# Down projections of a hybrid encoder layer: pair 17 multiplied in seven block products in the first run too, with its token sums made ahead of that run's eighth pair and the run's order rearranged

## The chip, the cores and the metric

The kernel runs on one core of one Trainium2 chip. The metric is the device time of one execution, in microseconds (us). The profile comes from one further execution of the same program, whose span is measured from the trace and whose own time is given beside it. Engines are named as the profile names them: PE multiplies matrices (PEld is its weight load), DVE and ACT are the vector and the scalar engine, POOL and SP issue DMA transfers here.

## The reference, cut to what matters

The layer has two feed-forward blocks of one form, one at its beginning and one at its end, and the change touches the second matrix product (the "down projection") of both.

```python
def swiglu(x, w_gate_up, w_down):
    gate, up = jnp.split(x @ w_gate_up, 2, axis=-1)
    return (jax.nn.silu(gate) * up) @ w_down
...
ff = swiglu(rms_norm(x, pre_norm_ffn1[layer]), w_ffn1_gate_up[layer], w_ffn1_down[layer])
x = x + 0.5 * rms_norm(ff, post_norm_ffn1[layer])
```

There are 256 tokens, the model width is 2048 and the hidden width is 5632, all in float32. So `w_down` is 5632 x 2048 and the product has 256 x 2048 results. Between the two feed-forward blocks lie a gated linear recurrence and a windowed attention, which the change leaves alone.

## The kernel before, in words

**Three products for one.** A float32 operand is split into a high part and a low part (`h` and `l`): ACT casts the tile to the high part (L177) and DVE subtracts it from the original to get the low part (L178). One product of two blocks is then three matmuls (high by high, high by low, low by high), which `Blocks.three` issues. All of them stand at line L458 in the profile. Each multiplies 128 x 128 weights into 512 columns.

**Pairs and runs.** `hts` holds the hidden activations: 22 tiles ("pairs"), each of two 128-row slices, already split into high and low. The down projection is done in two runs over these 22 pairs: run 0 makes the output columns 0 to 1023, run 1 the columns 1024 to 2047. For each pair and run, one raw tile of `w_down` (2 x 128 rows by 1024 columns, 1024 KB) is loaded, split and multiplied. The order of the pairs is written out by hand in the table `orders` (L1276), one list for each run. A place in that list is called a position here; position 6 is the seventh pair of a run, and pair 12 stands there.

**Plain and seven.** A pair is a 2 x 2 block of activations by a 2 x 2 block of weights. A plain pair takes eight block products, so 24 matmuls; its raw tile is split in two halves (two casts on ACT, two subtractions on DVE). A pair "in seven" takes seven block products, so 21 matmuls, by a scheme of the Strassen kind (`Blocks.products`, L505). It needs sums of the activation blocks ("token sums", tile `sums` or `su`, split into `sp`), and sums of the weight blocks in place of some weight blocks. Its first block is split alone (`ha`, `la`, from `one_block`, three of them at a time), then the lower half, then two weight sums are made on DVE (L1342 and L1343), then the upper half and once more the lower half are split (here "upper" and "last").

**Where the other weight sums come from.** For a pair listed in the table `added` (L1281), `prepare` (L1310) is called four positions ahead: it splits the first block and then has POOL issue a transfer of 512 KB (L1314) which adds the right-hand weight blocks onto the raw tile in flight. A pair in seven that is not in `added` makes these sums on DVE (L1337).

**Token sums.** Pairs 0, 2, ..., 18 are `MIXED`, and go in seven in both runs. For pairs 0 to 14 the token sums are made in the stage before. For 16 and 18, `sums_again` (L1103) makes them during run 0, after the products of positions 8 and 14. It is five instructions on DVE (L1107, and four small ones L1111 to L1114). Pair 17 is plain in run 0; its sums are made after the products of index 24, that is the third pair of run 1, and it goes in seven in run 1 alone.

**Raw tiles and their loads.** Five raw tiles go round. When a pair's last half is split, `load_down` (L1293, transfer L1298 on SP) fills the tile with the next pair of a list that is sorted by position, with pairs of `added` pulled forward by 3.5 positions (L1283). Eight activation tiles (pairs 0 to 7) were put away in device memory in the stage before and are fetched back into four slots (`fetch`, L1139) at fixed positions (`fetch_at`).

**The order on the engines.** The whole stage is under a manual schedule: each engine runs its instructions as the code writes them. Step i of the loop at L1401 writes the split of position i + 1, then `prepare` of position i + 4 and the fetches, then the products of position i, then the rest of the split, then token sums due there. So DVE and ACT work ahead of PE; five `h` tiles and five `l` tiles (`hip`, `lop`) bound by how much.

Of the kernel before, what the change touches and what calls it, by code (L numbers as in the profile page):

```python
# [37 lines left out]
def hymba_layer_kernel(  # L38
# [37 lines left out]
    def nm(s):  # L76
        uid[0] += 1
        return f"{s}_{uid[0]}"
# [120 lines left out]
    def close_far():  # L199
        far["cm"].__exit__(None, None, None)  # L200
# [719 lines left out]
    def post_pool():  # L920
        return tc.tile_pool(name=nm("post"), bufs=4, reuse_waits="tile")
# [17 lines left out]
    MIXED = range(0, 20, 2)  # L939
# [142 lines left out]
    def ffn(gated, w_dn, post_gain, again, gain=None, lead=None, aside=None):  # L1082

        with ExitStack() as st:
# [6 lines left out]
            hts, sums, away = [], {}, {}  # L1091
# [98 lines left out]
            def some(steps, n):  # L1190
                for _ in range(n):
                    next(steps)
# [47 lines left out]
            def first_pairs(g, waiting):  # L1240

                gated.group(g)
                some(waiting, 1)
                gated.prepare(g, MIXED_IN[1])
                some(waiting, 1)
                ahead = gated.splits(g, 1)
                some(ahead, 2)
                gated.prepare(g, MIXED_IN[2])
                for one in gated.take(g, 0):
                    one()  # L1250
                some(waiting, 1)
                ahead = gated.splits(g, 2)
                some(ahead, 2)
                some(waiting, 1)
                some(ahead, 1)
                for one in gated.take(g, 1):
                    one()

            def pair_ahead(g, u):

                ahead = gated.splits(g, u + 1)
                next(ahead)
                if u + 1 == MIXED_IN[1]:
                    gated.prepare(g, MIXED_IN[3])
                next(ahead)
                for one in gated.take(g, u):
                    one()
                for _ in ahead:
                    pass
                if g == 1 and u == 5:  # L1270
                    sums_in(MIXED_IN[3])
                if u == 5 and 1 < g <= AWAY // 2 + 1:
                    put_away(2 * g - 4)
                    put_away(2 * g - 3)

            orders = [  # L1276
                [9, 11, 8, 13, 10, 15, 12, 1, 0, 3, 14, 5, 16, 17, 2, 7, 4, 19, 6, 18, 20, 21],

                [2, 7, 4, 9, 6, 8, 11, 10, 13, 12, 17, 15, 0, 5, 14, 3, 16, 1, 18, 19, 20, 21],
            ]  # L1280
            added = {0: (12, 0, 14, 16, 2, 4, 6, 18), 1: (*MIXED, 17)}  # L1281
            steps = [(r, u) for r in range(2) for u in orders[r]]
            in_order = sorted(  # L1283
                (i - 3.5 if u in added[r] else i, i) for i, (r, u) in enumerate(steps)
# [3 lines left out]
            rows = None  # L1288

            def as_seven(r, u):  # L1290
                return u in MIXED or r == 1 and u in added[1]

            def load_down(raw):  # L1293
                if coming and (coming[0] < NU + 19 or any(raw is one for one in gated.lasting)):
# [56 lines left out]
            def products(i, among=None):  # L1351
                r, u = steps[i]
                rows.pos = i - r * NU
                del raws[i]
                if as_seven(r, u):
                    rows.products(u, firsts.pop(i), *got.pop(i))
                else:
                    rows.play(u, *zip(*got.pop(i)), among)
                rows.pos += 1
# [3 lines left out]
            with tc.manual_schedule():  # L1363
                gated.prepare(1, MIXED_IN[0])
                some(gated.splits(1, 0), 2)
                for g in range(1, NG):
                    first_pairs(g, waiting)
                    for u in range(2, last - 1):
                        pair_ahead(g, u)
                    some(gated.splits(g, last), 2)  # L1370
                    if g < NG - 1:
                        gated.prepare(g + 1, MIXED_IN[0])
                    for one in gated.take(g, last - 1):
                        one()
                    boundary(g, gated.splits(g + 1, 0) if g < NG - 1 else splits(0))
                    waiting = units(gated.c, rest)
                    some(waiting, 2)
                room_cm.__exit__(None, None, None)
                close_far()
                back_cm = tc.tile_pool(name=nm("hb"), bufs=AWAY // 2, reuse_waits="tile")  # L1380
                back = back_cm.__enter__()
                fetch_at = {2: (1,), 3: (0,), 5: (3,), 6: (5,), 9: (2,), 10: (7,), 11: (4,), 13: (6,)}
                fetch_at.update({25: (0,), 26: (5,), 28: (3,), 29: (1,)})
                again_at = {8: 16, 14: 18, 24: 17}
                for u in MIXED[8:]:
                    sums[u] = None
                rows = Pairs(w_dn, orders, hts, sums, work, post_gain, near=MIXED[:2])
                rows.firsts = 3
                some(waiting, 2)
                ahead = splits(1)  # L1390
                some(ahead, 2)
                products(0)
                for _ in range(2):
                    load_down(back.tile([P, 2048], F32, tag="raw", name=nm("raw"), bufs=2))
                some(waiting, 1)
                ahead = splits(2)
                some(ahead, 2)
                some(waiting, 1)
                some(ahead, 1)
                products(1)  # L1400
                for i in range(2, 2 * NU - Pairs.HELD):  # L1401
                    if i == NU + 18:
                        back_cm.__exit__(None, None, None)
                        early_cm.__exit__(None, None, None)
                        post = rows.post = st.enter_context(post_pool())
                    ahead = splits(i + 1)
                    next(ahead, None)
                    prepare(i + 4)
                    for u in fetch_at.get(i, ()):
                        fetch(u)  # L1410
                    next(ahead, None)
                    if i == NU + 18:
                        rows.hold(1, raws[2 * NU - 2])
                    products(i)
                    for _ in ahead:
                        pass
                    if i in again_at:
                        sums[again_at[i]] = sums_again(again_at[i])
                    if i == 8:
                        rows.half_gain(far["pool"])  # L1420
                    if i == NU - 1:
                        sums[17] = None
                        rows.second_run()
                        rows.fold_after(NU - Pairs.HELD - 1)
                fold = rows.fold()
                some(fold, 2)
                rows.hold(1, raws[2 * NU - 1])
                for _ in fold:
                    pass
# [121 lines left out]
    def again_from(src):  # L1551
# [6 lines left out]

    kvbanks = [pa(), pa()]
    xt = ffn(  # L1560
        gated,
        w_ffn1_down[0],
# [818 lines left out]
```

## Time and profile before

| what | value |
|---|---|
| time, median of 3 runs | 1815.16 us (1814.6 to 1816.67) |
| profiled execution, its own time | 1816.97 us |
| its span | 1815.2 us |
| PE busy | 1802.6 us, 99% of the span, 8412 matmuls |
| DVE busy | 1645.7 us, 91% |
| ACT busy | 1128.2 us, 62% |
| POOL busy | 177.9 us, 10% |
| granted PE clock | 9 tenths or more in all 40 slices; mean 0.999 |
| HBM traffic | 251 GB/s over the span |
| down projection of the first feed-forward block, on PE | 476.5 to 702.9 us |
| down projection of the second, on PE | 1580.8 to 1806.7 us |

A matmul's duration in the profile (0.39 us) is longer than the distance to the next one, since they overlap in the array; what a matmul costs is read from how many start in a stretch of time. A busy PE is therefore no proof that it runs at its peak. The transfer times are from issue to landing. Idle time of an engine is listed with what ended it.

### The profile page before, as it was taken

The numbers are of one execution on the slowest core, as the hardware profiler recorded it, in microseconds if no ns is written. First come the engines' busy times: TensorE is split into PE (matmuls) and PEld (weight loads), VectorE is DVE, ScalarE is ACT, GpSimd is POOL, SyncE is SP. The second block draws the span as 40 slices with busy tenths as digits, with TensorE's granted clock in tenths as the row PEclk, the third lists the DMA queues.
The fourth block names the chain that finished last, engine by engine and source line by source line (L and its number), as shares of the span: only waits on it lengthen the run. The fifth ranks groups of instructions, "written<-read, shape, count | busy, mean of one in ns | idle before, by whom it ended". The sixth has DMA issues, their size and how long they took to land.

```text
span 1815.2 us, 23684 instructions
## 1 busy us (share of the span) xinstructions
PE 1802.6 (99%) x8412; PEld 1496.8 (82%) x8412; DVE 1645.7 (91%) x2149; ACT 1128.2 (62%) x1496; POOL 177.9 (10%) x168
## 2 busy tenths in 40 slices
PE   9999999999999999999999999999999999999998
PEld 7888888888888888888888888888888888888886
DVE  7999999999989988988888888899999999998987
ACT  7565666666565757556676666566666666566663
POOL 1011111111011100110000100111111111011110
PEclk9999999999999999999999999999999999999999
DMA  8889999999699996965655767889999998699994
GB/s 302 240 237 282 276 283 255 254 257 260 212 343 279 280 323 208 296 174 163 174 162 166 245 206 276 244 244 270 284 268 272 255 249 251 192 337 311 263 315 164
DMA packets 217335, 457.06 MB, mean 252 GB/s; under 512 B 13064, under 2 KB 49760, under 8 KB 215936
## 3 DMA queue, kind: packets, MB, share of 16 engines
q1 hardware_dynamic: 181600, 389.07, 61.6%
q0 software_dynamic: 35440, 66.21, 21.4%
q8 instruction: 66, 1.08, 0.2%
q14 instruction: 53, 0.43, 0.1%
q10 hardware_dynamic: 176, 0.27, 0.0%
HBM read 440.80 MB, written 14.70 MB: 251 GB/s over the span
## 4 chain that ended last, share of the span: by engine, by line
PE 88%; DMA 4%; DVE 4%; ACT 2%; issue 1%; SPq 0%; POOL 0%; DVEq 0%; ACTq 0%; POOLq 0%
PE pa L458 40%; PE pb L458 35%; PE pa L326 5%; PE pa L331 3%; DMA raw<-in_w_ffn_gate_up_dram 2%; DVE l L178 2%; DMA raw<-in_w_mix_in_dram 2%; ACT h L177 1%; PE pb L1728 1%; PE pa L1172 1%; PE pb L1172 1%; DMA vr<-in_w_mix_in_dram 1%; PE pa L381 0%; ACT xt L228 0%; PE pa L380 0%
## 5 line engine op out<-in xcount | busy, mean ns | idle before, releaser
L177 ACT CAST h<-raw 128x1024 fp32r<-128x1024 f32 (+1 forms) x846 | 833.0, 1011 | 455.7 <-PE pb L458 152.4
L178 DVE TENSOR_TENSOR l<-raw,h 128x1024 fp32r<-128x1024 f32 (+1 forms) x846 | 963.0, 1170 | 97.6 <-ACT h L177 79.1
L458 PE MATMUL pa<-h,xt 128*128 128x512 f32 x1194 | 418.9, 392 | 0.1
L458 PE MATMUL pb<-h,xt 128*128 128x512 f32 x1038 | 371.0, 392 | 0.4 <-DVE pb L1229 0.4
L458 PEld LDWEIGHTS pa<-h,xt 128*128 128x128 f32 x1194 | 224.2, 188 | 47.9 <-DVE xt L233 0.6
L458 PE MATMUL pa<-l,xt 128*128 128x512 f32 x597 | 233.1, 390 | 0.4 <-DVE l L178 0.4
L458 PEld LDWEIGHTS pb<-h,xt 128*128 128x128 f32 x1038 | 194.8, 188 | 46.5 <-DVE pb L1236 3.7
L458 PE MATMUL pb<-l,xt 128*128 128x512 f32 x519 | 202.3, 390 | 0.0
L1011 POOL DMA_DIRECT2D raw<-in_w_ffn_gate_up_dram x78 | 94.5, 1212 | 733.0 <-DVE l L178 656.9
L458 PE MATMUL pb<-h,ht 128*128 128x512 f32 x452 | 159.2, 389 | 0.0
L458 PE MATMUL pa<-h,ht 128*128 128x512 f32 x452 | 159.2, 389 | 0.0
L458 PEld LDWEIGHTS pa<-l,xt 128*128 128x128 f32 x597 | 112.2, 188 | 23.4 <-DVE l L178 1.7
L458 PE MATMUL pa<-h,xs 128*128 128x512 f32 x332 | 118.6, 389 | 0.0
L458 PE MATMUL pb<-h,xs 128*128 128x512 f32 x332 | 115.7, 389 | 0.0
L458 PEld LDWEIGHTS pb<-l,xt 128*128 128x128 f32 x519 | 97.5, 188 | 18.7
L326 PE MATMUL pa<-xt,h 128*128 128x512 f32 x448 | 109.9, 393 | 0.0
L458 PEld LDWEIGHTS pa<-h,ht 128*128 128x128 f32 x452 | 84.9, 188 | 17.7
L458 PEld LDWEIGHTS pb<-h,ht 128*128 128x128 f32 x452 | 84.8, 188 | 17.7
L326 PEld LDWEIGHTS pa<-xt,h 128*128 128x128 f32 x448 | 81.5, 188 | 15.3
L458 PE MATMUL pa<-l,ht 128*128 128x512 f32 x226 | 87.9, 389 | 0.0
L458 PE MATMUL pb<-l,ht 128*128 128x512 f32 x226 | 87.9, 389 | 0.0
L1314 POOL DMA_DIRECT2D raw<-in_w_ffn_down_dram x38 | 46.1, 1212 | 371.7 <-DVE la L178 320.7
(341 smaller groups left out, 2537.8 us busy)
## 6 DMA issues: line engine op xcount, KB each, us to landing
raw<-in_w_ffn_gate_up_dram SPq DMA_DIRECT2D x350, 512.0 KB, 5.9
raw<-in_w_ffn_down_dram SPq DMA_DIRECT2D x88, 1024.0 KB, 8.1
raw<-in_w_ffn_gate_up_dram POOLq DMA_DIRECT2D x78, 512.0 KB, 8.0
raw<-in_w_mix_in_dram SPq DMA_DIRECT2D x36, 1024.0 KB, 5.1
raw<-in_w_ffn_down_dram POOLq DMA_DIRECT2D x38, 512.0 KB, 10.3
ht<-away SPq DMA_DIRECT2D x24, 512.0 KB, 10.4
raw<-in_w_mix_out_dram SPq DMA_DIRECT2D x12, 1024.0 KB, 6.5
raw<-in_w_mix_in_dram SPq DMA_DIRECT2D x34, 256.0 KB, 5.3
```

The lines of the kernel that those rows point to most:

```text
L177: nc.scalar.copy(hi, src)
L178: nc.vector.tensor_tensor(lo, src, hi.bitcast(F32), ALU.subtract)
L326: nc.tensor.matmul(slot[f], weights(hs, kk, f), xcol(xt, k), start=(k == 0), stop=(k == KT - 1))
L331: nc.tensor.matmul(slot[f][:, 0:T], weights(ls, kk, f), xcol(xt, kh * 8 + kk, 0), start=False, stop=False,)
L458: nc.tensor.matmul(self.bank(at), lhs, rhs, start=(n == 1), stop=n in (ends, self.of[at]), skip_group_check=n > ends,)
L1011: nc.gpsimd.dma_start(raw[:, 0:1024].rearrange("p (k c) -> p k c", k=2), self.source(u, g)[:, :, 1], accum_op=ALU.add,)
L1172: nc.tensor.transpose(bank[:, o : o + P], zs[m][:, k * P : (k + 1) * P], ident)
L1314: nc.gpsimd.dma_start(raws[i][:, 0:1024].rearrange("p (k c) -> p k c", k=2), Pairs.part(w_dn, u, r)[:, :, 512:1024], accum_op=ALU.add,)
L1728: nc.tensor.matmul(dst, left[a], right[b], start=first and i == 0, stop=last and i == 2)
```

## The change

Pair 17 joins `added[0]`, so it goes in seven in run 0 as well as in run 1. Its token sums are now made after the products of position 4 of run 0 (while position 6, pair 12, is still to be split), and stay until run 1, where they are no longer made. In the order of run 0, pair 17 moves from position 13 to position 7, behind pair 12; pairs 1, 0, 3, 14, 5 and 16 each come one position later, and pairs 2 and 7 change places. From position 16 on nothing moves, and the order of run 1 is as it was. `as_seven` asks only the table now. It holds for both feed-forward blocks.

```diff
             orders = [
-                [9, 11, 8, 13, 10, 15, 12, 1, 0, 3, 14, 5, 16, 17, 2, 7, 4, 19, 6, 18, 20, 21],
+                [9, 11, 8, 13, 10, 15, 12, 17, 1, 0, 3, 14, 5, 16, 7, 2, 4, 19, 6, 18, 20, 21],
...
-            added = {0: (12, 0, 14, 16, 2, 4, 6, 18), 1: (*MIXED, 17)}
+            added = {0: (12, 17, 0, 14, 16, 2, 4, 6, 18), 1: (*MIXED, 17)}
...
             def as_seven(r, u):
-                return u in MIXED or r == 1 and u in added[1]
+                return u in added[1]
...
-                again_at = {8: 16, 14: 18, 24: 17}
-                for u in MIXED[8:]:
+                again_at = {4: 17, 8: 16, 14: 18}
+                for u in (*MIXED[8:], 17):
                     sums[u] = None
...
                     if i == NU - 1:
-                        sums[17] = None
                         rows.second_run()
```

By the sorting rule the raw tiles of run 0 were loaded in the order of pairs 9, 11, 8, 12, 13, 10, 0, 15, 14, 1, 16, 3, 2, 5, and are now loaded in the order 9, 11, 8, 12, 13, 17, 10, 15, 0, 14, 1, 16, 3, 2, 5.

The first place is DVE in run 0, from the halves of pair 15 (position 5) to pair 12 (position 6). Before: `raw_642` is pair 15, `raw_645` pair 12, `la_4381` the first block of pair 0.

```order
L178 TENSOR_TENSOR l_4377<-raw_642,h_4376 128x1024
L178 TENSOR_TENSOR la_4381<-raw_4221,ha_4380 128x512
L178 TENSOR_TENSOR l_4386<-raw_642,h_4385 128x1024
L178 TENSOR_TENSOR l_4412<-raw_645,h_4411 128x1024
L178 TENSOR_TENSOR sp_4415<-sums_750,sp_4415 128x4x128
L1342 TENSOR_TENSOR raw_645<-raw_645 128x512
L1343 TENSOR_TENSOR raw_645<-raw_645 128x512
L178 TENSOR_TENSOR l_4423<-raw_645,h_4422 128x1024
L178 TENSOR_TENSOR l_4451<-raw_645,h_4450 128x1024
```

Now, behind the second half of pair 15: `su_4411` are the token sums of pair 17, `la_4427` is the first block of pair 0.

```order
L1107 TENSOR_TENSOR su_4411<-ht_3566 128x512
L1111 TENSOR_TENSOR su_4411<-su_4411 128x128
L1112 TENSOR_TENSOR su_4411<-su_4411 128x128
L1113 TENSOR_TENSOR su_4411<-su_4411 128x128
L1114 TENSOR_TENSOR su_4411<-su_4411 128x128
L178 TENSOR_TENSOR l_4418<-raw_645,h_4417 128x1024
L178 TENSOR_TENSOR sp_4421<-sums_750,sp_4421 128x4x128
L1342 TENSOR_TENSOR raw_645<-raw_645 128x512
L1343 TENSOR_TENSOR raw_645<-raw_645 128x512
L178 TENSOR_TENSOR la_4427<-raw_639,ha_4426 128x512
L178 TENSOR_TENSOR l_4434<-raw_645,h_4433 128x1024
L178 TENSOR_TENSOR l_4462<-raw_645,h_4461 128x1024
```

The five instructions of the token sums stand between pair 15 and pair 12, and the first block of pair 0 has moved into pair 12.

The second place follows on it on DVE. Before, pair 1 (`raw_4219`, plain) came behind pair 12, with the first block of pair 14 (`la_4460`) between its halves, and then pair 0.

```order
L178 TENSOR_TENSOR l_4456<-raw_4219,h_4455 128x1024
L178 TENSOR_TENSOR la_4460<-raw_639,ha_4459 128x512
L178 TENSOR_TENSOR l_4467<-raw_4219,h_4466 128x1024
L178 TENSOR_TENSOR l_4493<-raw_4221,h_4492 128x1024
L178 TENSOR_TENSOR sp_4496<-sums_750,sp_4496 128x4x128
```

Now pair 17 (`raw_4219`) comes behind pair 12, and then pair 1 (`raw_642`).

```order
L178 TENSOR_TENSOR l_4467<-raw_4219,h_4466 128x1024
L178 TENSOR_TENSOR sp_4470<-su_4411,sp_4470 128x4x128
L1342 TENSOR_TENSOR raw_4219<-raw_4219 128x512
L1343 TENSOR_TENSOR raw_4219<-raw_4219 128x512
L178 TENSOR_TENSOR l_4478<-raw_4219,h_4477 128x1024
L178 TENSOR_TENSOR l_4503<-raw_4219,h_4502 128x1024
L178 TENSOR_TENSOR l_4508<-raw_642,h_4507 128x1024
L178 TENSOR_TENSOR la_4512<-raw_4221,ha_4511 128x512
L178 TENSOR_TENSOR l_4517<-raw_642,h_4516 128x1024
```

Two pairs in seven now stand one behind the other, and DVE does the six instructions of pair 17 ahead of pair 1.

The third place is ACT near the end of run 0, at the first block of pair 18 (position 19), with the engines whose semaphores each row waits for. Before, `ha_4831` is that block and `h_4822` the lower half of pair 4.

```order
L177 CAST h_4822<-raw_645 128x1024 [waits PE_49,Activation_49]
L177 CAST sp_4826<-sums_750 128x4x128
L177 CAST ha_4831<-raw_639 128x512 [waits DMAHW3_49]
L177 CAST h_4836<-raw_645 128x1024 [waits DMASW7_49,DVE_49,PE_49]
L177 CAST h_4864<-raw_645 128x1024 [waits DVE_49,PE_49,Activation_49]
```

Now `ha_4851` is that block, and `h_4842` the lower half of pair 4.

```order
L177 CAST h_4842<-raw_4219 128x1024 [waits PE_49,Activation_49]
L177 CAST sp_4846<-sums_750 128x4x128
L177 CAST ha_4851<-raw_645 128x512 [waits DMAHW3_49,PE_49]
L177 CAST h_4856<-raw_4219 128x1024 [waits DMASW0_49,Activation_49]
L177 CAST h_4881<-raw_4219 128x1024 [waits DVE_49,PE_49,Activation_49]
```

The first block of pair 18 has a wait for PE that it had not: the three tiles for first blocks are then held by pairs 2, 4 and 6, and it takes the one of pair 2, which PE frees with that pair's first product.

## The prediction

> **What bounds the kernel now.** I read the page first: the span, the busy shares and the chain that ended last by engine.
>
> ```profile
> span 1815.2 us, 23684 instructions
> PE 1802.6 (99%) x8412; PEld 1496.8 (82%) x8412; DVE 1645.7 (91%) x2149; ACT 1128.2 (62%) x1496; POOL 177.9 (10%) x168
> PE 88%; DMA 4%; DVE 4%; ACT 2%; issue 1%; SPq 0%; POOL 0%; DVEq 0%; ACTq 0%; POOLq 0%
> ```
>
> PE is busy nearly throughout and carries 88% of the chain, but DVE is close behind, and this change takes work from PE and gives work to DVE. So I asked the windows for the middle of each run of the first down projection, and the waits for that stage (480 to 700 us).
>
> ```profile
> core 0: us, PE busy (x) PEld busy (x) DVE busy (x) ACT busy (x) POOL busy (x), PEclk, DMA share, GB/s
> 500.00:580.00 80.00, 80.00 (x354) 66.26 (x354) 72.00 (x85) 50.63 (x59) 9.71 (x8) 1.00 0.99 315
> 600.00:680.00 80.00, 80.00 (x355) 66.26 (x354) 72.29 (x82) 50.84 (x58) 9.70 (x8) 1.00 1.02 321
> ```
>
> ```profile
> DVE l L178 <- ACT h L177: 15.7, 18, 2.5
> ACT h L177 <- DMA raw<-in_w_ffn_down_dram: 8.1, 8, 2.7
> PEld pa L458 <- DVE y L713: 0.3, 1, 0.3
> ```
>
> Run 0 and run 1 start equally many matmuls, 354 and 355 in 80 us: one each 80/354 = 0.226 us at the full clock. PE's only wait in the list is 0.3 us. DVE and ACT do wait (for each other and for transfers), and DVE idles 8 us of 80. So the stage runs at PE's issue rate, and the cover is how far DVE's low parts are ready ahead of PE, which I call the lead.
>
> **The change part by part.**
>
> *PE.* Pair 17 goes from 24 matmuls to 21 in run 0, in two feed-forward blocks: 6 x 0.226 = 1.36 us less. The order shows it: PE has 8160 rows in place of 8166. All of it is on the path, because PE sets the pace there.
>
> *DVE and ACT.* A pair in seven costs DVE more than a plain one. The chain in run 1, where the token sums of 17 stand now, has every piece, and moreover in the very order that the change makes in run 0: sums of 17, a pair in seven (6), a first block, a second pair in seven (8), a plain pair (11).
>
> ```profile
> 604.53 0.69 DVE L1107 TENSOR_TENSOR su<-ht 128x512 f32<-128x512 f32 x1
> ...
> 606.44 1.22 DVE L178 TENSOR_TENSOR l<-raw,h 128x1024 fp32r<-128x1024 f32 x1
> 607.58 0.69 DVE L178 TENSOR_TENSOR sp<-sums,sp 128x512 fp32r<-128x512 f32 x1
> 608.18 0.69 DVE L1342 TENSOR_TENSOR raw<-raw 128x512 f32<-128x512 f32 x1
> 608.90 0.69 DVE L1343 TENSOR_TENSOR raw<-raw 128x512 f32<-128x512 f32 x1
> 609.51 0.68 DVE L178 TENSOR_TENSOR la<-raw,ha 128x512 fp32r<-128x512 f32 x1
> 610.11 3.49 DVE L178 TENSOR_TENSOR l<-raw,h 128x1024 fp32r<-128x1024 f32 x3
> 613.52 0.68 DVE L178 TENSOR_TENSOR sp<-sums,sp 128x512 fp32r<-128x512 f32 x1
> 614.12 0.69 DVE L1342 TENSOR_TENSOR raw<-raw 128x512 f32<-128x512 f32 x1
> 614.84 0.69 DVE L1343 TENSOR_TENSOR raw<-raw 128x512 f32<-128x512 f32 x1
> 615.45 3.64 DVE L178 TENSOR_TENSOR l<-raw,h 128x1024 fp32r<-128x1024 f32 x3
> ```
>
> By distances between starts, the token sums take 606.44 - 604.53 = 1.9 us, and pair 17's additions 0.6 (first block), 0.6 (`sp`), 0.7 and 0.6 (weight sums), 1.1 (third half): 3.7 us. So run 0 gets 5.6 us more on DVE, and run 1 loses the 1.9. It is off the path while the lead lasts. In run 1 it lasted: the upper half of pair 8 was ready at 615.45 + 1.22 = 616.67, and PE used it at 617.88, 1.2 us later.
>
> ```profile
> 617.88 0.39 PE L458 MATMUL pa<-l,sp 128*128 128x512 f32 x1
> ```
>
> Now the same chain in run 0. These are DVE from the second half of pair 15 on, and PE at the first product of pair 12 and at the one behind its last.
>
> ```profile
> 501.02 2.35 DVE L178 TENSOR_TENSOR l<-raw,h 128x1024 fp32r<-128x1024 f32 x2
> 505.23 2.51 DVE L178 TENSOR_TENSOR l<-raw,h 128x1024 fp32r<-128x1024 f32 x2
> 509.10 1.23 DVE L178 TENSOR_TENSOR l<-raw,h 128x1024 fp32r<-128x1024 f32 x1 [1.37 <-ACT h L177]
> ```
>
> ```profile
> 508.65 0.39 PE L458 MATMUL pa<-ha,ht 128*128 128x512 f32 x1
> 513.41 0.39 PE L458 MATMUL pa<-h,ht 128*128 128x512 f32 x1
> ```
>
> The second half of 15 starts at 501.02. Ahead of it the first block of 17 comes in and that of pair 0 goes out, which cancels. But 17's raw tile is now loaded ahead of pair 10's. The two tiles issued at 481.3 and 481.7 landed as follows (the title of the row: minimum, median, maximum).
>
> ```profile
> DMA to landing us min/median/max: 7.8/8.8/9.8
> ```
>
> So pair 10 lands at 491.5 in place of 489.1. It can shift DVE's chain by 0 (a tile that waits anyway) to 2.4 us; I take 0.4, since the other first blocks before it fill most of that time. The sums then start at 501.02 + 1.14 + 0.4 = 502.6, and by run 1's distances pair 17's upper half is ready 616.67 - 604.53 = 12.1 us later, at 514.7. PE begins pair 17 at 513.41, and uses that half ten matmuls on, at 515.7. The lead is 1.0 us. For the last half it is 1.0 us too (515.98 against 517.03). No stall; with the shift of 2.4 us one of about 1 us in each stage.
>
> *Transfers.* The next tile in danger is pair 3's. Its load is issued when pair 17's last half is done, about 516.1. Here are the loads issued at 500 to 525 us, those of the same place in the second feed-forward block (1602 to 1630 us), and the adding transfers of POOL at 489 to 535 us; then ACT's and DVE's half of a tile.
>
> ```profile
> DMA to landing us min/median/max: 8.2/9.1/10.8
> DMA to landing us min/median/max: 7.5/9.5/10.4
> DMA to landing us min/median/max: 10.0/11.2/12.4
> ```
>
> ```profile
> L178 DVE TENSOR_TENSOR l<-raw,h 128x1024 fp32r<-128x1024 f32 x110 | 131.6, 1221 | 16.8 <-ACT h L177 15.7
> L177 ACT CAST h<-raw 128x1024 fp32r<-128x1024 f32 x109 | 112.7, 1051 | 79.6 <-DVE raw L1343 32.2 <-PE pb L458 19.3 <-PE pa L458 14.1
> ```
>
> Landed at 516.1 + 9.1 = 525.2, cast (1.05) and subtracted (1.22), with 0.1 estimated for each of two handovers, the first low part stands at 527.7. PE needs it 67 matmuls after 513.41, at 528.6. The lead is 0.9 us: the transfer may take 9.9 us before PE waits. At 10.8 the stall is 0.9 us. POOL's added transfer for 17 is issued behind its first block, three halves ahead of 15's second: 501.4 - 3 x 1.14 = 498.0. It is needed for 17's L1342, 614.12 - 604.53 = 9.6 behind the sums' start at 502.6, so at 512.2: 14.2 us for 12.4 at most.
>
> *What else moves.* Pairs 0 to 7 are fetched into four slots; the fetch of 2, written at step 9, now waits on SP for pair 1 at position 8 in place of 7. It is needed at position 15, six pairs of some 5 us later, and the load behind it on SP serves position 16, so it hurts nobody. Near the end of run 0, ACT's first block of pair 18 waits for PE's first product of pair 2, and pair 4's upper and last halves are queued behind it on ACT, for which DVE and then PE wait. Before, pair 4 began on PE at this time:
>
> ```profile
> 559.65 0.39 PE L458 MATMUL pa<-ha,ht 128*128 128x512 f32 x1
> ```
>
> It will begin 0.7 earlier, at 559.0, and pair 2 21 matmuls before it, at 554.2; its first product ends at about 555.0. Then come 0.6 (first block), 1.05 and 1.22: the upper half at 558.0, needed at 561.2. Free.
>
> *Sum.* The profiled execution took 1816.97 us, 1.8 around its span: 1816.97 - 1.36 = 1815.6. It lies 1.81 above the median of 1815.16, so the median comes to 1815.16 - 1.36 = 1813.8 us.
>
> **The rivals.** 0.2% of the time, about what a measurement of this kernel can tell from no change, is 3.63 us.
>
> *The slow transfer.* Pair 3's tile lands late, and PE waits for it in both blocks. One load in run 1 (issued 629.1) took this long, and ACT waited for it:
>
> ```profile
>   ACT h L177: 2.7, 1
> DMA to landing us min/median/max: 13.0/13.0/13.0
> ```
>
> At 13.0 us the price is 3.1 us in each stage: 2 x 3.1 - 1.36 = +4.8, so 1820.0. It decides from 9.9 + (3.63 + 1.36)/2 = 12.4 us on. For it: the stretch is full of transfers already, and 13 us did occur. Against: the loads at this very place took at most 10.8 and 10.4 us. 10%.
>
> *Transfers as the wall.* Each stage moves one more 512 KB (0.52 MB). Windows of 20 us around it:
>
> ```profile
> 520.00:540.00 20.00, 20.00 (x90) 16.58 (x89) 18.48 (x23) 11.90 (x15) 2.41 (x2) 1.00 1.04 350
> 580.00:600.00 20.00, 20.00 (x89) 16.30 (x89) 19.71 (x27) 11.39 (x19) 2.43 (x2) 1.00 0.73 222
> ```
>
> If the 350 GB/s were a wall that PE stands at, 0.52/350 is 1.5 us a stage: 2 x 1.5 - 1.36 = +1.6, so 1816.8. Against: PE started as many matmuls in that window as in the others, and by 580 us the rate is down to 222, so the bytes find room later. 12%. The Trainium skill (DMA: Bandwidth & Descriptors, Where 436 GB/s comes from) says that the HBM side binds such loads at about 358 GB/s for a core. The trace's 350 agrees that little is left there; by that figure the estimate would be the same +1.6.
>
> *More than the sum.* Run 1 is relieved of 1.9 us on DVE; with 0.3 us of PE waiting in the whole stage there is nothing to win by it. 3% for a gain over 3.63 us by something unseen. That pair 17 stays plain is excluded by the order.
>
> **How the numbers follow.** Forecast 75%: 1813.8 us, by itself 1812.6 (a run spread of 2.07 us, half to each side) to 1815.6 (both stages stall 0.9 us). The wall 12%, the slow transfer 10%, an unseen gain 3%. The range, 1812.6 to 1817.0, takes in the wall. Within 0.2% are the first two: 87%; slower 10%, faster 3%.
>
> **What would show it.** PE has 8406 matmuls, DVE 10 and ACT 6 instructions more, L1314 one issue more in each block. Right: windows of 500 to 580 us still start 354 matmuls; 17's upper half is ready about 1 us ahead of use; pair 3's load lands within 10 us. Wrong: PE waiting for `l` (L178) near 515 or 528 us, fewer than 350 matmuls in that window, or a load issued near 516 us that takes over 12 us.

## The result: slower by 4.4 us

The changed kernel takes 1820.22 us (median of 14 runs), the kernel before 1815.78 (14 runs on the same chip). Thirteen runs of the changed kernel lie between 1818.21 and 1822.6 us; the fourteenth was disturbed (4706.77 us) and is left out of the ratio. The ratio is 1.0024, 95% interval 1.0016 to 1.0033: slower by 0.24%, where 1813.8 was predicted and 1817.0 was the top of the range. Its profiled execution took 1819.26 us, that of before 1816.97.

The page of the changed kernel, in the lines that were shown of before (span; busy time of each engine; the chain that ended last by engine):

```profile
span 1817.5 us, 23697 instructions
PE 1802.4 (99%) x8406; PEld 1495.3 (82%) x8406; DVE 1651.7 (91%) x2159; ACT 1130.3 (62%) x1502; POOL 180.3 (10%) x170
PE 89%; DVE 6%; DMA 2%; issue 2%; ACT 1%; SPq 0%; DVEq 0%; ACTq 0%; POOL 0%; POOLq 0%
```

The instruction counts are as forecast: six matmuls fewer, ten instructions more on DVE, six on ACT, two on POOL. But PE's busy time fell by 0.2 us only, the span grew by 2.3, and DVE's part of the chain rose from 4% to 6%. The windows over the middle of each run (us, then busy time and count by engine, granted clock, DMA share, GB/s) and the waits between 480 and 700 us (in total, times, longest) say where:

```profile
500.00:580.00 80.00, 77.99 (x343) 63.83 (x342) 73.65 (x91) 49.51 (x59) 9.71 (x8) 1.00 0.98 305
600.00:680.00 80.00, 80.00 (x354) 66.24 (x353) 70.95 (x78) 49.97 (x57) 9.71 (x8) 1.00 0.97 308
```

```profile
ACT h L177 <- DMA raw<-in_w_ffn_down_dram: 7.6, 4, 4.0
ACT ha L177 <- DMA raw<-in_w_ffn_down_dram: 7.5, 4, 2.9
PEld pa L458 <- DVE l L178: 3.0, 3, 2.4
PE pa L458 <- DVE l L178: 2.0, 1, 2.0
```

Run 0 starts 343 matmuls in its 80 us where 354 were started before. Run 1 starts as many as before, less one. From PE's first start to its last, the first down projection takes 229.1 us (475.4 to 704.5), where it took 226.4, and the second 227.2 (1581.8 to 1809.0), where it took 225.9. Together that is 4.0 us more, so the loss lies in the two down projections; the rest of this execution was 1.7 us shorter than in that of before. PE now waits for DVE's low parts, and ACT waits 7.5 us for tiles at its first blocks (`ha`), which before did not stand in the list.

**The chain at pair 17 held.** DVE's low parts of the upper half of 17 (first of three) and of pair 3, PE's first use of each, and the landing of pair 3's tile, which was issued at 514.5:

```profile
511.95 3.64 DVE L178 TENSOR_TENSOR l<-raw,h 128x1024 fp32r<-128x1024 f32 x3
524.63 1.22 DVE L178 TENSOR_TENSOR l<-raw,h 128x1024 fp32r<-128x1024 f32 x1
```

```profile
514.63 0.39 PE L458 MATMUL pa<-l,sp 128*128 128x512 f32 x1
527.55 0.39 PE L458 MATMUL pa<-l,ht 128*128 128x512 f32 x1
```

```profile
DMA to landing us min/median/max: 7.0/7.0/7.0
```

The leads are 514.63 - 513.17 = 1.5 us and 527.55 - 525.85 = 1.7 us. Nothing stalls there.

**The stall is 30 us later**, at positions 14 to 16 (pairs 7, 2, 4). These are the landing times of pair 7's tile (issued 533.1) and pair 6's (issued 536.0), each with ACT's wait for it (us, times):

```profile
  ACT h L177: 4.0, 1
DMA to landing us min/median/max: 12.4/12.4/12.4
```

```profile
  ACT ha L177: 2.9, 1
DMA to landing us min/median/max: 16.0/16.0/16.0
```

And here is how these waits reach PE, in the timelines of ACT, DVE and PE (the idle time before a row stands in brackets):

```profile
545.61 2.95 ACT L177 CAST h<-raw 128x1024 fp32r<-128x1024 f32 x3 [4.02 <-DMA raw<-in_w_ffn_down_dram]
551.97 0.62 ACT L177 CAST ha<-raw 128x512 fp32r<-128x512 f32 x1 [2.89 <-DMA raw<-in_w_ffn_down_dram]
```

```profile
546.69 3.50 DVE L178 TENSOR_TENSOR l<-raw,h 128x1024 fp32r<-128x1024 f32 x3 [3.55 <-ACT h L177]
555.86 0.69 DVE L1107 TENSOR_TENSOR su<-ht 128x512 f32<-128x512 f32 x1
561.44 2.35 DVE L178 TENSOR_TENSOR l<-raw,h 128x1024 fp32r<-128x1024 f32 x2
```

ACT waits 4.0 us for pair 7 and then 2.9 us for the first block of pair 6, which stands ahead of pair 2's last halves in its queue. DVE idles 3.6 us, must then still make the token sums of 18 (from 555.86), and has the upper half of pair 4 ready at 562.7. PE starts nothing for 2.4 us, of which its row counts 2.0 as idle:

```profile
560.08 0.62 PE L458 MATMUL pa<-h,sp 128*128 128x512 f32 x2
562.71 0.50 PE L458 MATMUL pa<-l,sp 128*128 128x512 f32 x1 [2.01 <-DVE l L178]
```

### The profile page after: what moved, and what is told of

It is laid out like the page before. It is cut to its first block, busy times and chain, and to the rows that moved or that the text cites. A ratio compares the mean times of both kernels' runs of the same rounds, so it can differ in the third digit from the quotient of the medians.

```text
span 1817.5 us, 23697 instructions
## 1 busy us (share of the span) xinstructions
PE 1802.4 (99%) x8406; PEld 1495.3 (82%) x8406; DVE 1651.7 (91%) x2159; ACT 1130.3 (62%) x1502; POOL 180.3 (10%) x170
## 3 DMA queue, kind: packets, MB, share of 16 engines
q1 hardware_dynamic: 181600, 389.07, 61.5%
## 4 chain that ended last, share of the span: by engine, by line
PE 89%; DVE 6%; DMA 2%; issue 2%; ACT 1%; SPq 0%; DVEq 0%; ACTq 0%; POOL 0%; POOLq 0%
PE pa L458 40%; PE pb L458 35%; PE pa L326 5%; PE pa L331 3%; DVE l L178 3%; DMA raw<-in_w_ffn_down_dram 1%; ACT h L177 1%; PE pa L381 1%; PE pa L380 1%; PE pa L379 1%; PE pb L1727 1%; PE pa L1172 1%; PE pb L1172 1%; PE pb L2028 0%; DVE raw L1342 0%
## 5 line engine op out<-in xcount | busy, mean ns | idle before, releaser
L458 PE MATMUL pa<-h,ht 128*128 128x512 f32 x440 | 155.3, 390 | 0.3
L458 PE MATMUL pb<-h,ht 128*128 128x512 f32 x440 | 155.2, 389 | 0.0
```

What stands on the lines that cost most here:

```text
L458: nc.tensor.matmul(self.bank(at), lhs, rhs, start=(n == 1), stop=n in (ends, self.of[at]), skip_group_check=n > ends,)
```

## The experiments: which resource was full

All runs compare with the kernel before on the same chip (1815.7 to 1816.3); the two numbers in brackets are the 95% interval of the ratio. The expectations call DVE VectorE, ACT ScalarE and SP SyncE. The first four ask whether the order, the place of an operation or the late tiles make the loss. LATE TILE takes the tiles for the cause; TOO MUCH ON DVE takes DVE's additional instructions for it.

**The order alone** (`added[0]` without 17, `as_seven` and the sums of 17 as before):

```
-            added = {0: (12, 17, 0, 14, 16, 2, 4, 6, 18), 1: (*MIXED, 17)}
+            added = {0: (12, 0, 14, 16, 2, 4, 6, 18), 1: (*MIXED, 17)}
-                again_at = {4: 17, 8: 16, 14: 18}
+                again_at = {8: 16, 14: 18, 24: 17}
```

> The new order of run 0 alone: pair 17 stays plain in run 0 and its token sums are made in run 1 again, but pairs 2 and 4 stand one behind the other as in the changed kernel. Two theories. LATE TILE: one more pulled-forward load among five raw tiles makes pair 6's tile be issued a step later (536 us against 532) into a crowd of transfers; it landed 16.0 and 14.6 us after issue, ACT is in order and was held 2.9 and 3.7 us at that pair's first block, ahead of pair 2's upper half, and PE stalls at pair 4. TOO MUCH ON DVE: pairs 2 and 4 in seven, with the token sums of pair 18 between them, are more than DVE can do, whatever the transfers. LATE TILE expects about the time of before, ratio 1.000 (no PE wait over 0.5 us at pair 4). TOO MUCH ON DVE expects the stall of the changed kernel without its saving: 5 to 6 us more than before, ratio 1.003.

Measured: 1816.12, ratio 1.000 [0.9991, 1.0009]. Pairs 2 and 4 next to each other and the later fetches cost nothing by themselves.

**The token sums of 18 two steps later:**

```
-                again_at = {4: 17, 8: 16, 14: 18}
+                again_at = {4: 17, 8: 16, 16: 18}
```

> The changed kernel with pair 18's token sums made after position 16 in place of position 14, so that their 1.9 us no longer stand between pairs 2 and 4 on DVE. TOO MUCH ON DVE expects the stall at pair 4 gone and the saving of 1.36 us seen: ratio to before 0.9993. LATE TILE expects ACT's hold at the first block of pair 6 to stay at 3 to 4 us and pair 2's upper half to be as late as in the changed kernel, but the stall at pair 4 smaller by up to 1.9 us in each block: ratio 1.000 to 1.001.

Measured: 1819.56, 1.002 [1.0011, 1.0029]. PE no longer waits at pair 4, but it waits 0.3 us at 577 us and 1.4 us at 586 us, the end of run 0; in all it idles 2.0 us there where the changed kernel idles 2.4. Both theories expected less: that place is not the cause.

**The first block of pair 6 behind pair 2's halves** (at step 14 `prepare(i + 4)` follows the rest of `ahead`):

```
-                    prepare(i + 4)
+                    if i != 14:
+                        prepare(i + 4)
...
+                    if i == 14:
+                        prepare(i + 4)
```

> The changed kernel with the first block of pair 6 (and POOL's adding transfer for it) written behind pair 2's last half in place of ahead of its upper half, so that a late tile of pair 6 holds nothing of pair 2. DVE has the same work in the same stretch. LATE TILE expects pair 2's halves 3 us earlier, no stall over 0.5 us at pair 4, ratio to before 0.9993 to 1.000. TOO MUCH ON DVE expects the stall at pair 4 unchanged, 1 to 2.5 us in each block, ratio 1.002.

Measured: 1816.74, 1.0006 [0.9997, 1.0015], with runs from 1814.6 to 1820.7. ACT's queue passes the late tile on to PE, but the tile was nearly as late (14.5 us): the edit treats the symptom, and not in every run. The interval fits LATE TILE (up to 1.000) better than TOO MUCH ON DVE (1.002).

**Two fetches fewer** (pairs 7 and 4 use the activations of 5 and 2 in run 0, so that part isn't computed):

```
-10: (7,), 11: (4,), 13: (6,)}
+13: (6,)}
```

> The changed kernel without the fetches of pairs 7 and 4 in run 0 (the activations of pairs 5 and 2 are used in their place), so 1 MB less between 528 and 548 us. LATE TILE expects pair 6's tile to land in 10 to 13 us in place of 15 to 16, ACT's hold at its first block under 1 us, and the stall at pair 4 gone: ratio to before 0.9993. TOO MUCH ON DVE expects no difference from the changed kernel: ratio 1.002 to 1.003.

Measured: 1814.34, 0.9993 [0.9984, 1.0002]; pair 6's tile lands in 10.0 us, as LATE TILE expected. The median agrees with the 1.4 us of six matmuls fewer, though the interval still takes in no change. So the crowd of transfers is where the loss comes out. What crowds them was open, since the order alone moves nearly the same bytes. The next four separate the added transfer from DVE's added work.

**Seven products without the adding transfer** (17 stays in seven; its weight sums on DVE, its tile in its plain place):

```
+            landed = {0: (12, 0, 14, 16, 2, 4, 6, 18), 1: added[1]}
-                i - 3.5 if u in added[r] else i
+                i - 3.5 if u in landed[r] else i
...
-                if i < len(steps) and steps[i][1] in added[steps[i][0]]:
+                if i < len(steps) and steps[i][1] in landed[steps[i][0]]:
```

> Pair 17 stays in seven products in the first run, but its weight sums are made on VectorE and not by an adding transfer, and its tile keeps its plain place among the loads: 0.5 MB less to move, about 1.3 us more on VectorE. CROWDED TRANSFERS (the tiles of pairs 7 and 6 land late because too much is asked of the transfers at once): these two tiles land in 8 to 11 us again, gaps of TensorE in the first run back to about 0.3 us, time 1814.5 to 1816. VECTORE BEHIND (VectorE's additional work of some 4 us per first run makes every load be issued 2 to 3 us late, and this alone makes them late): VectorE has more to do than in the changed kernel, the two tiles are issued later still, time 1820 to 1823.

Measured: 1823.03, 1.0038 [1.0026, 1.0051]. With 0.5 MB less to move in each down projection it is slower still; pair 6's tile takes 15.1 us. CROWDED TRANSFERS by bytes alone falls. The run can't price the adding transfer by itself, because DVE got its work (about 1.3 us) in exchange.

**Without the token sums of 17** (those of 12 in their place, so that part of the result isn't computed):

```
-                        sums[again_at[i]] = sums_again(again_at[i])
+                        u = again_at[i]
+                        sums[u] = sums[12] if u == 17 else sums_again(u)
```

> The changed kernel without making pair 17's token sums at the fifth position (those of pair 12 are used in their place in both runs, so part of the result is not computed): about 1.9 us less on VectorE, all transfers as in the changed kernel. CROWDED TRANSFERS: the tile of pair 6 still takes 14 to 16 us, gaps of TensorE of 2 to 3.5 us per first run, time 1818 to 1820. VECTORE BEHIND: the loads go out about 2 us sooner, the tile of pair 6 lands before it is wanted, time 1815 to 1816.

Measured: 1814.57, 0.9995 [0.9986, 1.0004], 1813.8 to 1818.3. The profiled execution is one of the longest (1818.27), and in it pair 6's tile still took 15.2 us: 1.9 us less on DVE takes the loss away in most runs, not in all. The median is where VECTORE BEHIND had it (1815 to 1816), or a little below; the profiled execution is one as CROWDED TRANSFERS had it (1818 to 1820).

**The fetches of 4 and 6 one step later:**

```
-10: (7,), 11: (4,), 13: (6,)}
+10: (7,), 12: (4,), 14: (6,)}
```

> The changed kernel with the fetch of the activations of pair 4 one step later (behind the load of pair 6 in SyncE's queue instead of ahead of it), and that of pair 6 one step later as well; all work is done. CROWDED TRANSFERS: the load of pair 6 shares the engines with 0.5 MB less, so it lands some 1.5 to 3 us sooner, the stall at pair 4 shrinks from 2 us and more to below 1 us, time 1815 to 1817.5. VECTORE BEHIND: the loads are issued when they were, time 1819 to 1821.

Measured: 1816.26, 1.0002 [0.9994, 1.0011]; pair 6's tile in 11.5 us. It gives 4 us back, as CROWDED TRANSFERS had it and VECTORE BEHIND (1819 to 1821) had not.

**Only the tile of 17 loaded ahead** (on top of the order alone, 17 plain):

```
-                i - 3.5 if u in added[r] else i
+                i - 3.5 if u in added[r] or (r, u) == (0, 17) else i
```

> The new order with pair 17 plain in the first run (which cost nothing by itself, 1816.1), and only its tile loaded ahead of its turn as in the changed kernel: no adding transfer, no products fewer. If the tile taken ahead is what leaves the later loads short: tiles of pairs 7 and 6 in 12 to 16 us and time 1818 to 1820. CROWDED TRANSFERS by bytes alone, or VECTORE BEHIND: 1816 to 1816.5, tiles in 8 to 11 us.

Measured: 1816.34, 1.000 [0.9991, 1.0009]. Loading ahead costs nothing.

The last four test the two causes from the other side.

**The order alone, and more work for DVE** (17 plain; its token sums made three times over in run 0, and not again in run 1):

```
+                    if i in (4, 5, 6):
+                        sums[17] = sums_again(17)
```

> The new order with pair 17 plain in the first run (1816.1 by itself), and only work for VectorE added: pair 17's token sums made three times over, at the fifth, sixth and seventh position (about 5.6 us; the changed kernel has 4.7 us more than the order alone between 483 and 540 us). No transfer and no product is changed. VECTORE BEHIND: the loads of pairs 5, 4, 7 and 6 go out 2 to 3 us later, the tiles of 7 and 6 take 11 to 16 us, TensorE stalls by 1 to 3.5 us per first run, time 1818 to 1823. If VectorE's work alone is not the cause: 1816 to 1817.

Measured: 1819.46, 1.0020 [1.0011, 1.0028]. This is the decisive run: no product and no transfer differs from the order alone (1816.12), and 3.3 us are lost. That is not all of it: the changed kernel is 4.1 us above the order alone and should have been 1.4 below it. Landing times of the tiles of pair 7 and of pair 6, first for the order alone, then with more work for DVE (there with ACT's waits):

```profile
DMA to landing us min/median/max: 8.8/8.8/8.8
...
DMA to landing us min/median/max: 11.1/11.1/11.1
```

```profile
  ACT h L177: 2.9, 1
DMA to landing us min/median/max: 10.8/10.8/10.8
...
  ACT ha L177: 3.6, 1
DMA to landing us min/median/max: 15.1/15.1/15.1
```

VECTORE BEHIND expected all these loads 2 to 3 us later. Here are the issues on SP of the loads of pairs 4 and 7, and of pair 6 (the first of two in its row), first for the order alone, then with more work for DVE; both stages begin on PE at 474.8 to 474.9 us.

```profile
525.27 0.38 SPq L1298 DMA_DIRECT2D raw<-in_w_ffn_down_dram  x1
531.66 0.38 SPq L1298 DMA_DIRECT2D raw<-in_w_ffn_down_dram  x1
535.47 7.22 SPq L1298 DMA_DIRECT2D raw<-in_w_ffn_down_dram  x2
```

```profile
527.04 0.38 SPq L1298 DMA_DIRECT2D raw<-in_w_ffn_down_dram  x1
532.53 0.38 SPq L1298 DMA_DIRECT2D raw<-in_w_ffn_down_dram  x1
535.41 7.22 SPq L1298 DMA_DIRECT2D raw<-in_w_ffn_down_dram  x2
```

Pair 4's load goes out 1.8 us later and pair 7's 0.9, but pair 6's goes out at the same time and still lands 4 us later: it meets loads ahead of it that were pushed together. From the start of the stage, the changed kernel issues these three loads within 0.1 us of the times of this run.

**The token sums of 17 on GpSimd** (all five instructions of `sums_again` by `add`), and **those of 16, 17 and 18, with the later fetches** (there the tuple is `(16, 17, 18)`):

```
+                add = (nc.gpsimd if u in (17,) else nc.vector).tensor_tensor
-                nc.vector.tensor_tensor(a22, a21, a22, ALU.subtract)
+                add(a22, a21, a22, ALU.subtract)
```

> The changed kernel with pair 17's token sums made on GpSimd instead of VectorE at the same place (an add of this size took 1.26 us there and 0.69 us on VectorE, so about 3 us in GpSimd's free time ahead of the adding transfer of pair 0); all work is done. VECTORE BEHIND: VectorE has 1.9 us less in front of pairs 5, 7 and 4, as in the run without these sums: 1814.5 to 1816.5. If the seven products' transfers are what holds the kernel: 1819 to 1821. If GpSimd's work delays the adding transfer of pair 0 or slows VectorE's adds: 1817 to 1822, with VectorE's busy time grown in the stretch.

> The changed kernel with the token sums of pairs 16, 17 and 18 made on GpSimd in both down projections, and the fetches of pairs 4 and 6 one step later; all work is done. VECTORE BEHIND, with the crowd of transfers as its effect: VectorE gains 5.6 us per first run, the loads have room, nothing is left of the stall, and the 1.4 us of six products fewer are seen: 1814 to 1815.3, faster than before. If GpSimd delays its adding transfers or shares a path with VectorE: 1816 to 1820.

Measured: 1822.77 (1.0031 [1.0019, 1.0044]) and 1825.22 (1.0049 [1.0037, 1.0062]). Both are above every range that was given. DVE got fewer instructions and was slower at the others. GpSimd's first and last sum and its adding transfer for pair 0, and DVE's five low parts beside the sums:

```profile
498.69 1.79 POOL L1108 TENSOR_TENSOR su<-ht 128x512 f32<-128x512 f32 x1
504.78 1.32 POOL L1115 TENSOR_TENSOR su<-su 128x128 f32<-128x128 f32 x1
508.98 1.23 POOL L1315 DMA_DIRECT2D raw<-in_w_ffn_down_dram  x1 [2.88 <-DVE la L178]
```

```profile
497.22 8.55 DVE L178 TENSOR_TENSOR l<-raw,h 128x1024 fp32r<-128x1024 f32 x5
```

Five subtractions take 8.55 us, 1.71 each, where they stand 1.14 apart elsewhere: nearly 3 us lost to spare 1.9. The adding transfer had waited 2.9 us for DVE, so it was DVE and not GpSimd's sums that held it up.

**Both cures that kept all work,** the later fetches and the first block of 6 behind pair 2:

```
-10: (7,), 11: (4,), 13: (6,)}
+10: (7,), 12: (4,), 14: (6,)}
...
-                    prepare(i + 4)
+                    if i != 14:
+                        prepare(i + 4)
...
+                    if i == 14:
+                        prepare(i + 4)
```

> The changed kernel with the two fetches one step later and, besides, the first block of pair 6 and its adding transfer behind the halves of pair 2 instead of ahead of them, so that ScalarE no longer holds pair 2 up while it waits for pair 6's tile; all work is done. VECTORE BEHIND, with the late tile of pair 6 as the place where it comes out: each of the two edits alone gave 3.5 to 4 us back (1816.3 and 1816.7); if they act on the same stall together they leave 0.5 us of it or less and the 1.4 us of six products fewer are seen: 1814.4 to 1815.5. If VectorE's backlog only comes out at another place (a stall at the last pairs of the run, or at the first pairs of the second run): 1816 to 1818.

Measured: 1817.14, 1.0005 [0.9996, 1.0014]. Not better than either alone: the stall at pair 4 is gone in the profile, but PE's next matmul comes 0.3 us late at 584 us and 0.4 us late at 591 us (there behind DVE), as it does in the changed kernel, and again in the second block. Four times some 0.35 us is as much as the 1.4 us to be won. No version that does all the work beat the kernel before.

**What the traces say together.** The stretches 483 to 540 us (ahead of the stall) and 540 to 600 us, in the columns of the windows above; the order alone:

```profile
483.00:540.00 57.00, 57.00 (x253) 47.20 (x252) 50.45 (x60) 34.56 (x41) 6.08 (x5) 1.00 1.02 341
540.00:600.00 60.00, 60.00 (x266) 49.46 (x265) 57.49 (x71) 38.53 (x51) 8.41 (x7) 1.00 0.88 265
```

The kernel before (its first stretch):

```profile
483.00:540.00 57.00, 57.00 (x253) 47.19 (x252) 53.19 (x62) 36.19 (x43) 6.08 (x5) 1.00 1.03 343
```

The changed kernel, and the order alone with more work for DVE:

```profile
483.00:540.00 57.00, 57.00 (x253) 47.20 (x252) 55.20 (x69) 35.68 (x44) 7.28 (x6) 1.00 1.02 335
540.00:600.00 60.00, 57.64 (x250) 46.35 (x249) 55.08 (x68) 36.89 (x49) 7.29 (x6) 1.00 0.88 269
```

```profile
483.00:540.00 57.00, 57.00 (x253) 47.22 (x252) 55.21 (x75) 34.52 (x41) 6.08 (x5) 1.00 0.98 324
540.00:600.00 60.00, 58.82 (x258) 47.73 (x257) 55.60 (x68) 36.05 (x49) 7.29 (x6) 1.00 0.89 273
```

Seven products without the adding transfer, and two fetches fewer (the first stretch only):

```profile
483.00:540.00 57.00, 57.00 (x253) 47.05 (x252) 54.68 (x68) 34.40 (x43) 6.08 (x5) 1.00 0.97 318
```

```profile
483.00:540.00 57.00, 57.00 (x253) 47.22 (x252) 55.97 (x70) 36.53 (x44) 7.35 (x7) 1.00 1.03 335
```

Two resources are full here, not one. The order alone leaves DVE 57 - 50.45 = 6.5 us of idle time in the first stretch; the changed kernel leaves 1.8, and the same order with nothing but DVE work added leaves 1.8 too. (The kernel before had 3.8.) By the kernel, a tile's next load goes out only when its last half is split, so a late DVE lets the transfers' engines run below what they did (share 0.98 and 0.97 against 1.02), and that time is missing when the fetches and the loads of 7 and 6 come. The other resource is these engines themselves: with two fetches fewer, DVE is fullest of all (55.97), and PE does not wait.

One can estimate it in time of the transfers' engines. The page of before gives their queues: packets, MB, share of the span.

```profile
q1 hardware_dynamic: 181600, 389.07, 61.6%
q0 software_dynamic: 35440, 66.21, 21.4%
```

By this a plain load costs 0.158% of the span per MB, an adding transfer 0.323%: 0.52 MB of the latter takes 0.52 x 0.00323 x 1815 = 3.1 us of all engines, as much as a plain load of twice the size (1.05 MB: 3.0 us). A fetch (0.52 MB) takes 1.5 us. These are averages over the whole execution; the stretch 483 to 540 us of before alone, where the first row is GB/s in 40 slices, gives a ratio of 2.1:

```profile
GB/s 428 400 411 420 394 207 394 379 290 285 290 293 309 378 400 253 295 303 295 296 381 420 421 295 306 285 367 413 302 263 341 368 413 388 417 394 338 308 302 296
q1 hardware_dynamic: 4470, 17.04, 78.6%
q0 software_dynamic: 1281, 2.49, 24.0%
```

The arrears at 540 us, against the order alone, are then (1.02 - share) x 57 plus 3.1 where 17's adding transfer was due, less what was left out or put behind the load of pair 6. A share is rounded to 0.01, so each figure is uncertain by some 0.3 us:

| kernel | share | arrears, us | PE idle 540 to 600, us | median, us |
|---|---|---|---|---|
| order alone | 1.02 | 0 | 0 | 1816.12 |
| tile of 17 loaded ahead | 1.01 | 0.6 | 0.2 | 1816.34 |
| two fetches fewer | 1.03 | -0.5 | 0 | 1814.34 |
| order alone, more on DVE | 0.98 | 2.3 | 1.2 | 1819.46 |
| without sums of 17 | 1.03 | 2.5 | 1.3 | 1814.57 (profiled 1818.27) |
| later fetches | 1.00 | 2.7 | 1.1, and 0.2 before | 1816.26 |
| seven, no adding transfer | 0.97 | 2.9 | 2.5 | 1823.03 |
| changed kernel | 1.02 | 3.1 | 2.4 | 1820.22 |
| sums of 18 later | 1.02 | 3.1 | 2.0 | 1819.56 |
| three sums on GpSimd, later fetches | 0.99 | 3.3 | 3.4, and 0.4 before | 1825.22 |
| sums of 17 on GpSimd | 1.00 | 4.2 | 2.4, and 1.0 before | 1822.77 |

The two kernels with pair 6's first block moved are not in it, since there another instruction waits. Arrears below 1 us are absorbed; from 2 us on PE idles for about half of them up to a little more than all. The sums were made after the runs, so they describe them and were not tested on a further one. (The medians hold both feed-forward blocks and many executions, the other columns the first block of one, so they follow each other only roughly: the later fetches left no gap in the second block of the profiled execution, and the three kernels above 1822 us lost time to the clock there, as told at the end.) So the runs show two parts of the cause: DVE's added work (added by itself it costs 3.3 us, and 1.9 us less of it mends most runs), and transfers so full behind it that they can't catch up (two fetches fewer mend it, later ones give most of it back). Together they put the loads of the run's last third about 3 us in arrears by the estimate, at a place with no cover. That the adding transfer of 17 makes up the rest of the loss is only reckoned: no run adds it or takes it away with DVE's work unchanged. LATE TILE named the place where the loss comes out, and was wrong on what makes the tiles late; DVE's work is that, as TOO MUCH ON DVE and VECTORE BEHIND had it, but only beside full transfers. The size of the loss in a single execution stays open: the run without the sums of 17 took 1813.8 us in one execution and 1818.3 in another, and nothing here shows what decides between them.

## Why the prediction was wrong, point by point

- **PE, six matmuls x 0.226: right in number, and nothing contradicts the price.** PE has 8406 matmuls in place of 8412. With two fetches fewer the time was 1814.34 against 1816.14 of before on that chip, -1.8 where -1.36 was the sum, with an interval that takes in no change.
- **DVE's and ACT's chain at pair 17: right.** The lead of 1.0 us was 1.5; no stall.
- **Pair 3's load: right, and beside the point.** It took 7.0 us; 9.9 were allowed.
- **The step that failed is "It is off the path while the lead lasts", for the 5.6 us more on DVE.** I tested the lead at pairs 17 and 3, and let the work vanish after that. But DVE had been busy for 53.2 of the 57 us ahead of 540; work that doesn't stall at its own place stays as arrears until DVE idles again, and the loads behind it go out late and close together. From the start of the stage, the loads of pairs 2, 5, 4 and 7 were issued 3.4, 2.4, 1.8 and 0.9 us later than in the order alone; pair 6's was not, but its tile took 16.0 us in place of 11.1, and PE started nothing for 2.4 us. DVE's idle time there, 3.8 us of 57 before and 6.5 with the new order, was the number to charge the 5.6 us against; I had quoted 8 us of 80 for the stage and did not use it.
- **POOL's added transfer for 17, "14.2 us for 12.4 at most", was right as a deadline and left out the price.** The stretch at pair 17 shows no wait for it. I gave it 0.52/350 = 1.5 us in a rival; by the page's queues it takes an estimated 3.1 us of the engines.
- **"The fetch of 2 ... hurts nobody", and pair 4 "Free": failed.** The order alone confirms them for the order. For the whole change, pair 4's upper half was needed at about 560.5 and came at 562.7, because ACT stood behind pair 6's tile, a load that I had not looked at.
- **The rivals.** *The slow transfer* (1820.0, 10%) named the kind of event and the size: a tile that takes about 13 us, and 1820.2. It was put at pair 3's tile, whereas the tiles of pairs 7 and 6 took 12.4 and 16.0; and its evidence against ("at most 10.8 and 10.4 us") came from the kernel before, in which DVE was not behind. That its 1820.0 comes so near is luck: it was summed from two stalls of 3.1 us at a tile that was on time. *Transfers as the wall* (1816.8) had the crowd but not the arrears of DVE. The rule of the Trainium skill cited there (DMA: Bandwidth & Descriptors, Where 436 GB/s comes from), that the HBM side binds such loads at about 358 GB/s, isn't what held: in the kernel before, slices of 1.4 us of the stretch reached 400 to 428 GB/s, and the changed kernel's mean there was 335, below the 341 of the order alone.
- **The range** came from the spread of the runs and one bounded stall (by its own working the lower end is 1813.8 - 1.04 = 1812.8, not 1812.6); a late tile was given one chance in ten because each load was judged by itself.

## What to carry to other kernels

When a change adds work to an engine that frees buffers, charge it against that engine's idle time from there to the next long wait, and then ask which loads are issued later and what the loads behind them meet; a lead that holds at the changed place says nothing about thirty microseconds on. Price a transfer by the engine time that its kind takes on the page, not by its bytes. And a run that only adds the suspected work to an unharmed kernel can settle what removing things leaves open.

## What the hardware did that I had not expected

- An adding transfer cost the transfers' engines 2.0 times as much per byte as a plain load, on average over the execution (21.4% for 66.21 MB against 61.6% for 389.07 MB).
- GpSimd's f32 adds took 1.79 us at 128x512 where DVE's took 0.69, and 1.3 us at 128x128 where DVE's took 0.29; meanwhile DVE's subtractions came 1.71 us apart in place of 1.14. The Trainium skill (Perfetto Trace Analysis, Optimizing Scalar/DVE Operations) says that the two share a read port and that moving work between them might not help. The trace agrees, and shows that it can cost more than it spares (2.9 us against 1.9).
- A gap of 2.4 us on PE was followed, in the second feed-forward block of the run without the adding transfer, by matmuls at about half the clock (window 1671 to 1675 us):

```profile
1671.00:1675.00 4.00, 4.00 (x12) 3.13 (x11) 4.00 (x5) 3.05 (x4) 0.00 (x0) 0.57 0.93 150
```

The granted clock was 0.57 there: 12 matmuls started in 4 us, where at 0.226 us there would be 17 or 18. Both kernels with sums on GpSimd did the same after their gap of 2.4 us in the second block (0.51 from 1671.5 to 1674.8 us, and 0.58 from 1673 to 1677). Gaps of the same length in the first block of these three and of the changed kernel had no such sequel, and what decides it isn't shown. So a stall of this size can cost more than its own length: 0.43 x 4 = 1.7 us here, part of why this execution came out slower than the changed kernel.
